# A two-layer decoder trunk on one core: split VectorE sums, ScalarE draining two of eight PSUM banks, a fifth seven-product pair, and a re-ordered opening

## The chip, the cores and the metric

The kernel runs on one core of a Trainium2 chip. TensorE (PE) multiplies, with its weight loads shown as PEld; VectorE (DVE) and ScalarE (ACT) prepare operands and drain PSUM; GpSimd (POOL) and SyncE (SP) start DMA transfers. The metric is the time of one execution in microseconds of device time; lower is better.

## The reference

Two layers on a 256 x 2048 residual stream, all in float32:

```python
def hybrid_layer(x, ...):
    h = rms_norm(x, attn_norm)
    proj = einsum('bsd,de->bse', h, w_in)      # 2048 -> 6160 columns
    ... gated linear attention, stick-breaking attention, norms ...
    x = x + einsum('bse,ed->bsd', mixed, w_o)  # 2048 x 2048
    hm = rms_norm(x, mlp_norm)
    up = square(relu(einsum('bsd,df->bsf', hm, w_up)))   # 2048 x 8192
    return x + einsum('bsf,fd->bsd', up, w_down)         # 8192 x 2048
```

About 500 MB of weights pass once through the core.

## The kernel before

Every large product is done to float32 accuracy with three matmuls: a weight tile is split into a rounded part (`whi`, made by ScalarE at L1091) and the rest (`wlo`, made by VectorE at L1095), the activation likewise, and high x high, high x low and low x high are summed in PSUM (`product`, L1224, L1227, L1228). Below, "product" means one such triple.

Most of the work is a list of **units** (`layer_units`): per layer `g`, `o`, `o`, then four quarters of `up`, `up`, `down`, `down`, and ahead of a layer the three units `iv`, `ik`, `iq` of the next input projection. A unit multiplies 256 rows by a 2048 x 1024 weight block. It goes through eight **pairs** of 128-row weight slices in the order of a table (`EACH`, `OWN`, ...); the second entry of a table names its seven-product pairs, the third those whose split is done by DMA (`chi` by a GpSimd DMA, `dlo` a negated copy made by ScalarE at L1056, to which a second DMA adds the weights). A plain pair costs eight products. A seven-product pair (`fast`, the 2 x 2 Strassen-Winograd scheme) costs seven, but VectorE first forms sums of its weights (`ts`, `raw`, L871) and of its activations (`forms`, L464 to L467). Its products go to PSUM banks m1 to m8, which the unit's **tail** (`seeded_tail`, `up_tail`) adds up on VectorE.

`Plan` decides the order: each piece has a length, its dependences and a due time worked back from TensorE, and VectorE and ScalarE take the ready piece that is due first. The result is the in-order instruction stream of each engine; TensorE's own order is the tables'. In-order means that an instruction that waits holds up all that stand behind it on its engine.

The **opening** is not planned: `unit` runs one 512-column unit `u0` of the first layer (tiles `acc`, `ps`), loading x (`xb`) in four parts between the four weight loads (`raw`, 1 MB each). Then `ordered(-1, ...)` plans `iv`, `ik`, `iq` of layer 0. In the plan, time 0 is five steps (60 matmuls) ahead of the first `iv` product, and VectorE and ScalarE are taken to be free from then on. Weights come through a ring of `RAWS` = 3 `raw` tiles; the first three `chi` tiles are first touched by a one-element ScalarE copy (`held_tile`, L1047), which their DMAs wait for.

Of the kernel before, what the change touches and what calls it, by code (L numbers as in the profile page):

```python
# [14 lines left out]
ALU = mybir.AluOpType  # L15
# [16 lines left out]
OWN = {
    ("up", 0): ([4, 0, 0, 0, 0, 1, 1, 2, 1, 1, 6, 6, 2, 6, 6, 5, 5, 5, 5, 4, 3, 3, 3, 3, 7, 7], (0, 1, 3, 5, 6), (2, 4)),
    ("up", 0, 0): ([0, 0, 1, 1, 1, 4, 4, 1, 3, 3, 3, 6, 6, 3, 2, 6, 6, 5, 5, 5, 5, 2, 7, 7], FAST, (2, 4)),
    ("up", 1): ([0, 0, 3, 3, 3, 3, 2, 1, 1, 1, 2, 1, 5, 5, 5, 4, 6, 5, 6, 6, 6, 7, 4, 7], FAST, (2, 4)),
    ("down", 0): ([0, 0, 3, 3, 1, 2, 3, 3, 1, 1, 5, 1, 4, 5, 5, 5, 2, 6, 6, 6, 6, 7, 7, 4], FAST, (2, 4)),
    ("down", 1): ([0, 0, 5, 5, 4, 5, 5, 6, 6, 6, 4, 6, 3, 3, 3, 1, 2, 3, 1, 1, 1, 2, 7, 7], FAST, (2, 4)),
}
# [23 lines left out]
class Plan:  # L62
# [28 lines left out]
    def run(self):  # L91
# [32 lines left out]
        while events:  # L124
# [9 lines left out]
            for e in free:  # L134
# [38 lines left out]
def trunk_kernel(  # L173
# [275 lines left out]
    def forms(op, i, t, tag):  # L449
# [8 lines left out]

        def sums():
            a11, a21, a12, a22 = (t[:, k, r * P : (r + 1) * P] for k in range(2) for r in range(2))  # L460
            n = 4 if keep else 3
            e.append(tmp("t2", [P, 512], bufs=T2)[:, : n * P].rearrange("p (k c) -> p k c", c=P))
            s = e[0][:, 3, :] if keep else a21
            nc.vector.tensor_tensor(e[0][:, 2, :], a21, a11, ALU.subtract)  # L464
            nc.vector.tensor_tensor(s, a21, a22, ALU.subtract)
            nc.vector.tensor_tensor(e[0][:, 0, :], a11, s, ALU.subtract)
            nc.vector.tensor_tensor(e[0][:, 1, :], a12, e[0][:, 0, :], ALU.subtract)  # L467

# [386 lines left out]
    def ordered(l, units, hT, rst, ug, gates_t, mixed=None, ons=None):  # L855
# [147 lines left out]
        def load(u, i):  # L1003
# [4 lines left out]
            def fn():  # L1008
                if x % RAWS >= 3:
                    box.append(tmp("raw2", [P, 2, 1024], bufs=RAWS - 3))  # L1010
# [9 lines left out]
            if x >= RAWS:  # L1020
                piece.after = raws[x - RAWS]
            raws.append(readers)
# [12 lines left out]
        def rounded(u, j, s):  # L1035
# [252 lines left out]
        def seeded_tail(u):  # L1288
# [18 lines left out]
            def sums(p):  # L1307
# [6 lines left out]
                b = vector(dw, bk(7), dw, a, p[7])  # L1314
                d = vector(x22, bk(5), dw, b, p[5], seeds[8])
                free.update({1: [c], 6: [w], 5: [a, d], 7: [b]})
                box["s"] = (c, b, a, d)

            def half(c, p):
                got = []  # L1320
                for tt, (m, dst) in enumerate((((2, x11), (4, x21)), ((3, x12), (8, x22)))[c]):
                    def fn(m=m, dst=dst, tt=tt):
                        if m == 4:
                            combine(dst(), banks[m], dw(), ALU.subtract)
                        else:
# [4 lines left out]

                    before = [box["s"][2 * c + tt], seeds[m]] + [box["s"][3]] * (m == 4)
                    free[m] = [add("DVE", V1, fn, p[m], before, give=m == 4)]
                    got += free[m]
                x_done[2 * n2 + c] = got
# [3 lines left out]
        def up_tail(u):  # L1338
# [14 lines left out]
            def sums(p):  # L1353
                c = add("ACT", A1, copy, p[1])
                w = add("DVE", V1, new_dw, c, p[6], take=1, sure=1)
                a = vector(y(1, 0), bk(5), lambda: box["w"], w, p[5])
                b = vector(y(0, 1), bk(7), lambda: box["w"], w, a, p[7])
                b.give = 1
                d = vector(y(1, 1), bk(5), y(0, 1), b, p[5])
                free.update({1: [c], 6: [w], 5: [a, d], 7: [b]})  # L1360
                box["s"] = (c, b, a, d)

# [4 lines left out]
            def half(h, p):  # L1367
                box["r", h] = []
                for tt, m in enumerate(((2, 4), (3, 8))[h]):
                    minus = ALU.subtract if (h, tt) == (0, 1) else ALU.add  # L1370
                    before = [box["s"][2 * h + tt]] + [box["s"][3]] * ((h, tt) == (0, 1))
                    a = vector(y(h, tt), bk(m), y(h, tt), p[m], before, op=minus)
                    free[m] = [a]

# [557 lines left out]
```

## Time and profile before

| | |
|---|---|
| median of 3 runs | 2134.3 us (2134.24 to 2135.91) |
| the profiled execution | 2134.41 us, span 2132.7 us |
| busy: PE, PEld, DVE, ACT, POOL | 99%, 83%, 90%, 68%, 13% of the span |
| granted TensorE clock, mean | 0.999 of full speed |
| instructions: PE, DVE, ACT | 10064, 2578, 1940 |
| DMA | 497 MB, mean 233 GB/s |

The profiled execution is 1.7 us longer than its span and 0.1 us above the median. [...]

### The profile page before, as it was taken

What the parts mean: (1) busy time and instruction counts of PE and PEld (TensorE: products, weight loads), DVE (VectorE), ACT (ScalarE), POOL (GpSimd) and SP (SyncE); (2) the same over time, 40 slices, a digit from 0 to 9 for tenths busy, and PEclk for the clock granted to TensorE, in tenths of its full rate; (3) what the DMA queues carried; (4) which work ended last, traced back from release to release, by engine and by line L of the source; (5) the groups of instructions that cost most, each with busy time, mean ns of one, the idle gap of its engine ahead of it and who ended that gap; (6) DMA issues with size and microseconds to landing.
All of it is one profiled execution on the core that took longest, in us unless ns stands there. A gap on an engine that the chain in (4) does not pass through costs nothing.

```text
span 2132.7 us, 28217 instructions
## 1 busy us (share of the span) xinstructions
PE 2120.0 (99%) x10064; PEld 1763.6 (83%) x10064; DVE 1909.1 (90%) x2578; ACT 1452.1 (68%) x1940; POOL 276.4 (13%) x394
## 2 busy tenths in 40 slices
PE   8999999999999999999999999999999999999999
PEld 7888888888888888888888988888888888888887
DVE  5978779999999999999988896799999999999997
ACT  6657667676677677667766575677776776676774
POOL 1110001111111111111111100011112111111110
PEclk9999999999999999999999999999999999999999
DMA  8975358788988988988888644678889788889886
GB/s 257 259 227 174 115 176 242 223 255 243 271 245 244 268 245 245 283 244 234 250 261 245 192 138 138 213 217 244 264 241 272 234 262 256 240 246 273 242 245 200
DMA packets 157617, 497.14 MB, mean 233 GB/s; under 512 B 10682, under 2 KB 19458, under 8 KB 157476
## 3 DMA queue, kind: packets, MB, share of 16 engines
q1 hardware_dynamic: 100900, 319.16, 42.0%
q0 software_dynamic: 56576, 176.18, 36.9%
q8 instruction: 79, 1.29, 0.2%
q14 instruction: 62, 0.51, 0.1%
HBM read 493.20 MB, written 2.10 MB: 232 GB/s over the span
## 4 chain that ended last, share of the span: by engine, by line
PE 94%; DVE 3%; DMA 2%; ACT 1%; issue 1%; SPq 0%; ACTq 0%; DVEq 0%
PE acc L626 3%; PE acc L628 3%; PE acc L627 3%; DVE wlo L1095 1%; DMA xb<-in_x_dram 1%; DMA raw<-in_w_up_dram 1%; DMA raw<-in_w_in_dram 1%; PE ps L1869 0%; PE ps L1862 0%; DVE wlo L609 0%; PE ps L737 0%; PE ps L1819 0%; DVE ts L871 0%; PE ps L791 0%; PE ps L755 0%
## 5 line engine op out<-in xcount | busy, mean ns | idle before, releaser
L1095 DVE TENSOR_TENSOR wlo<-raw,whi 128x1024 fp32r<-128x1024 f32 (+1 forms) x689 | 744.0, 1089 | 86.2 <-ACT whi L1091 39.8
L1091 ACT ACTIVATE whi<-raw 128x1024 fp32r<-128x1024 f32 (+1 forms) x689 | 644.7, 950 | 185.8 <-DVE raw L871 67.6
L1056 ACT ACTIVATE dlo<-chi 128x1024 fp32r<-128x1024 f32 x168 | 177.6, 1057 | 117.7 <-DMA chi<-in_w_o_dram 5.1
L1091 ACT ACTIVATE whi<-ts 128x1024 fp32r<-128x1024 f32 x169 | 179.0, 1059 | 89.9 <-DVE ts L871 42.2
L871 DVE TENSOR_TENSOR ts<-raw 128x1024 f32<-128x1024 f32 x169 | 206.1, 1220 | 6.3 <-DMA raw<-in_w_o_dram 2.4
L1095 DVE TENSOR_TENSOR wlo<-ts,whi 128x1024 fp32r<-128x1024 f32 x169 | 206.1, 1220 | 4.1 <-ACT whi L1091 4.1
L626 PE MATMUL acc<-whi,act 128*128 128x512 f32 (+2 forms) x384 | 141.7, 369 | 1.6 <-ACT whi L607 1.6
L627 PE MATMUL acc<-wlo,act 128*128 128x512 f32 (+2 forms) x384 | 137.1, 357 | 0.2 <-DVE wlo L609 0.2
L628 PE MATMUL acc<-whi,act 128*128 128x512 f32 (+2 forms) x384 | 137.3, 358 | 0.0
L607 ACT ACTIVATE whi<-raw 128x1024 fp32r<-128x1024 f32 (+2 forms) x98 | 88.3, 906 | 69.2 <-PE acc L628 62.4
L609 DVE TENSOR_TENSOR wlo<-raw,whi 128x1024 fp32r<-128x1024 f32 (+2 forms) x98 | 100.3, 1030 | 32.5 <-ACT whi L607 32.3
L871 DVE TENSOR_TENSOR raw<-raw 128x512 f32<-128x512 f32 x169 | 116.2, 688 | 2.3
L871 DVE TENSOR_TENSOR raw<-ts,raw 128x512 f32<-128x512 f32 x169 | 115.8, 685 | 0.6
L1052 POOL DMA_DIRECT2D chi<-in_w_up_dram x64 | 38.0, 594 | 557.9 <-PE m__2856_13480 L1228 30.1
L1052 POOL DMA_DIRECT2D chi<-in_w_down_dram x64 | 38.8, 606 | 498.5 <-PE m__3324_15675 L1228 27.5
L1376 ACT ACTIVATE act<-act,st 128x512 f32<-128x512 f32 x88 | 60.2, 715 | 54.9 <-DVE act L871 54.9
L626 PEld LDWEIGHTS acc<-whi,act 128*128 128x128 f32 x384 | 72.6, 189 | 14.1 <-issue 3.4
L628 PEld LDWEIGHTS acc<-whi,act 128*128 128x128 f32 x384 | 72.7, 189 | 10.6
L627 PEld LDWEIGHTS acc<-wlo,act 128*128 128x128 f32 x384 | 72.8, 190 | 9.4 <-DVE wlo L609 0.5
L1059 POOL DMA_DIRECT2D dlo<-in_w_down_dram x64 | 60.1, 940 | 51.6 <-ACT dlo L1056 48.1
L1059 POOL DMA_DIRECT2D dlo<-in_w_up_dram x64 | 58.3, 912 | 55.9 <-ACT dlo L1056 53.6
L488 DVE TENSOR_TENSOR act<-t,act 128x512 fp32r<-128x512 f32 x92 | 62.7, 685 | 0.0
(4307 smaller groups left out, 5756.4 us busy)
## 6 DMA issues: line engine op xcount, KB each, us to landing
raw<-in_w_up_dram SPq DMA_DIRECT2D x96, 1024.0 KB, 7.4
raw<-in_w_down_dram SPq DMA_DIRECT2D x96, 1024.0 KB, 7.7
raw<-in_w_in_dram SPq DMA_DIRECT2D x72, 1024.0 KB, 5.7
chi<-in_w_up_dram POOLq DMA_DIRECT2D x64, 512.0 KB, 5.6
dlo<-in_w_up_dram POOLq DMA_DIRECT2D x64, 512.0 KB, 8.5
chi<-in_w_down_dram POOLq DMA_DIRECT2D x64, 512.0 KB, 5.6
dlo<-in_w_down_dram POOLq DMA_DIRECT2D x64, 512.0 KB, 8.5
raw<-in_w_o_dram SPq DMA_DIRECT2D x24, 1024.0 KB, 7.5
```

The lines of the kernel that those rows point to most:

```text
L488: nc.vector.tensor_tensor(d[:, :, 1, :], src, f32(d[:, :, 0, :]), ALU.subtract)
L607: newest["hi"] = nc.scalar.activation(h, r, AF.Copy).ins
L609: newest["lo"] = nc.vector.tensor_tensor(lo[:, q : q + step, :width], r, f32(h), ALU.subtract).ins
L626: nc.tensor.matmul(o, xh[:, sl], whi[:, j, :width], start=first, stop=False)
L627: nc.tensor.matmul(o, xh[:, sl], wlo[:, j, :width], start=False, stop=False)
L628: st["mm"] = nc.tensor.matmul(o, xl[:, sl], whi[:, j, :width], start=False, stop=last).ins
L871: nc.vector.tensor_tensor(dst, a, b, op)
L1052: nc.gpsimd.dma_start(flat("h"), src)
L1056: nc.scalar.activation(box["l"], f32(box["h"]), AF.Copy, scale=-1.0)
L1059: nc.gpsimd.dma_start(flat("l"), src, accum_op=ALU.add)
L1091: nc.scalar.activation(box["h"][:, :n], src(), AF.Copy)
L1095: nc.vector.tensor_tensor(box["l"][:, :n], src(), f32(box["h"][:, :n]), ALU.subtract)
```

## The change

Seven things are changed together. (1) Pair 0 becomes a seven-product pair in the second `down` unit of each quarter, whose table then has 26 steps instead of 24; the first `down` unit still uses pair 0 as a plain pair, so both forms of its activations are kept (`TWO_WAYS`, tile `sxk`; the `sxh` one moves to a tile of the `act` pool). (2) The four activation sums of `forms` become four planned pieces instead of one. (3) The planner counts 0.12 us between a VectorE piece and one that depends on it. (4) In both tails ScalarE copies banks m4 and m8 to SBUF, and VectorE adds there; the second read of bank m5 comes after the copy of m8. (5) In the opening the three `held_tile` copies read the last written element of `hT.t[7]`, the last operand of `u0`, instead of the identity, and the planner no longer makes them wait for its first step. (6) The opening's plan has a ring of six weight tiles. (7) Nearly all order tables are new.

```diff
-    ("down", 1): ([0, 0, 5, 5, 4, 5, 5, 6, 6, 6, 4, 6, 3, 3, 3, 1, 2, 3, 1, 1, 1, 2, 7, 7], FAST, (2, 4)),
+    ("down", 1): ([7, 7, 3, 3, 4, 3, 3, 5, 5, 5, 4, 5, 1, 1, 1, 1, 0, 0, 2, 0, 0, 6, 6, 6, 6, 2], (0, 1, 3, 5, 6), (2, 4)),
...
+FIRST_RAWS = 6
...
-                        at[u], free[e] + p.lag + (0.0 if u.engine == e else self.GAP)
+                        at[u], free[e] + p.lag + (self.SAME.get(e, 0.0) if u.engine == e else self.GAP)
...
             if tag_fast:
-                e = add("DVE", 1.25, lambda: part(0), first, take=1, sure=1 + got)
+                for k in range(4):
+                    kw = {} if k else dict(take=1, sure=1 + got)
+                    e = add("DVE", VS, lambda k=k: part(0, k), e, **kw)
...
-                nc.scalar.activation(box["h"][:, 0, :1], ident[:, :1], AF.Copy)
+                nc.scalar.activation(box["h"][:, 0, :1], f32(hT.t[7][:, 1, 1, :1]), AF.Copy)
...
-                first = add("ACT", 0.2, held_tile, before[0])
+                first = add("ACT", 0.2, held_tile)
...
-                d = vector(x22, bk(5), dw, b, p[5], seeds[8])
...
+                    if tt:
+                        free[m] = before = [add(
+                            "ACT", A1,
+                            lambda m=m, dst=dst: nc.scalar.activation(dst(), banks[m], AF.Copy),
+                            before,
+                        )]
+                    if m == 8:
+                        before = vector(x22, bk(5), x22, before, p[5])
+                        free[5] = free[5] + [before]
```

In the built programs TensorE has 24 matmuls fewer (9826 instructions instead of 9850), VectorE 80 instructions more and ScalarE 104 more. Two places matter below.

ScalarE, before, from the last square sums of the opening (`ssq`) on: the three `chi` copies stand at the very start of the program, and the first weight split of `iv` (`whi5`) comes before any `dlo`.

```order
L560 ACTIVATE t2_53_366,ssq_3_95<-xb3_94 128x512
L560 ACTIVATE t2_54_368,ssq_3_95<-xb3_94 128x512
L1091 ACTIVATE whi5_71_410<-raw_65_396 128x1024
L917 ACTIVATE act_55_382<-acc_13_145 128x512
L1056 ACTIVATE dlo_73_418<-chi_66_398 128x1024
```

The same place of the changed program:

```order
L564 ACTIVATE t2_53_366,ssq_3_95<-xb3_94 128x512
L564 ACTIVATE t2_54_368,ssq_3_95<-xb3_94 128x512
L1054 ACTIVATE chi_66_398<-act_43_304 128x1
L1054 ACTIVATE chi_67_400<-act_43_304 128x1
L1054 ACTIVATE chi_68_403<-act_43_304 128x1
L1063 ACTIVATE dlo_71_410<-chi_66_398 128x1024
L1063 ACTIVATE dlo_73_414<-chi_67_400 128x1024
L1098 ACTIVATE whi5_74_418<-raw_65_396 128x1024
L922 ACTIVATE act_55_382<-acc_13_145 128x512
```

The `chi` copies moved behind all ScalarE work of `u0`, and two `dlo` copies, which read what the `chi` DMAs bring, moved ahead of `whi5`.

VectorE, the end of the program (the last unit's tail; `xb3` is the last quarter of the output), before:

```order
L871 TENSOR_TENSOR xb3_94<-m5__4033_18993,t2_4072_19190 128x512
L871 TENSOR_TENSOR xb2_93<-m2__4014_18890,xb2_93 128x512
L871 TENSOR_TENSOR xb2_93<-m4__4018_18928,t2_4072_19190 128x512
L871 TENSOR_TENSOR xb3_94<-m3__4019_18930,xb3_94 128x512
L871 TENSOR_TENSOR xb3_94<-m8__4024_18956,xb3_94 128x512
```

and in the changed program:

```order
L876 TENSOR_TENSOR t2_4128_19428<-m7__4087_19205,t2_4128_19428 128x512
L876 TENSOR_TENSOR xb3_94<-m3__4072_19137,xb3_94 128x512
L876 TENSOR_TENSOR xb2_93<-xb2_93,t2_4128_19428 128x512
L876 TENSOR_TENSOR xb3_94<-m5__4084_19196,xb3_94 128x512
L876 TENSOR_TENSOR xb3_94<-xb3_94,t2_4128_19428 128x512
```

Bank m8 no longer appears here: ScalarE copies it to `xb3` first, and two dependent additions follow instead of one.

## Rows read from the trace of the kernel before

**Rows 1.** The page, busy time (share of the span) and instructions by engine.

```profile
PE 2120.0 (99%) x10064; PEld 1763.6 (83%) x10064; DVE 1909.1 (90%) x2578; ACT 1452.1 (68%) x1940; POOL 276.4 (13%) x394
```

**Rows 2.** Windows, one quarter: us, busy by engine (instructions), clock, DMA share, GB/s.

```profile
617.63:783.78 166.15, 166.15 (x752) 137.93 (x750) 156.85 (x194) 114.35 (x139) 24.75 (x32) 1.00 0.87 252
```

**Rows 3.** Windows of 20 us after the opening unit, same columns.

```profile
40.00:60.00 20.00, 18.89 (x81) 14.63 (x80) 18.43 (x24) 14.94 (x19) 3.72 (x5) 1.00 0.87 209
60.00:80.00 20.00, 19.92 (x87) 15.65 (x86) 19.32 (x31) 13.56 (x18) 3.68 (x5) 1.00 0.98 276
80.00:100.00 20.00, 20.00 (x90) 16.57 (x89) 19.90 (x24) 13.15 (x16) 1.40 (x2) 1.00 0.79 230
...
120.00:140.00 20.00, 18.93 (x83) 15.32 (x83) 19.24 (x24) 12.87 (x15) 1.41 (x2) 1.00 0.70 213
```

**Rows 4.** Timeline, the end: start, length, engine, line, operation [idle before <-releaser].

```profile
2119.10 0.60 ACT L1309 ACTIVATE xb<-m__4041_19027 128x512 f32<-128x512 f32 x1 [0.92 <-PE m__4041_19027 L1228]
...
2121.30 0.69 DVE L871 TENSOR_TENSOR t<-m__4034_18997,t 128x512 f32<-128x512 f32 x1
...
2122.03 0.69 DVE L871 TENSOR_TENSOR xb<-m__4033_18993,t 128x512 f32<-128x512 f32 x1
...
2122.30 0.39 PE L1224 MATMUL m__4024_18956<-chi,act 128*128 128x512 f32 x1
...
2128.20 0.39 PE L1228 MATMUL m__4024_18956<-whi,act 128*128 128x512 f32 x1
2128.62 0.69 DVE L871 TENSOR_TENSOR xb<-m__4024_18956,xb 128x512 f32<-128x512 f32 x1 [0.67 <-PE m__4024_18956 L1228]
```

**Rows 5.** Timeline of VectorE, two stretches without a gap.

```profile
36.10 0.28 DVE L464 TENSOR_TENSOR t<-act 128x128 f32<-128x128 f32 x1
36.30 0.28 DVE L465 TENSOR_TENSOR t<-act 128x128 f32<-128x128 f32 x1
...
46.72 1.22 DVE L1095 TENSOR_TENSOR wlo<-ts,whi 128x1024 fp32r<-128x1024 f32 x1
47.86 0.69 DVE L871 TENSOR_TENSOR raw<-raw 128x512 f32<-128x512 f32 x1
48.46 1.22 DVE L1095 TENSOR_TENSOR wlo<-raw,whi 128x1024 fp32r<-128x1024 f32 x1
```

**Rows 6.** The chain that ended last: start, us, what (two PSUM additions).

```profile
404.86 1.20 DVE xb L871 x2
```

**Rows 7.** Timeline of TensorE in the opening.

```profile
10.26 0.51 PE L626 MATMUL acc<-whi,act 128*128 128x512 f32 x1 [1.56 <-ACT whi L607]
...
11.91 0.63 PE L627 MATMUL acc<-wlo,act 128*128 128x512 f32 x1
...
14.89 0.48 PE L628 MATMUL acc<-whi,act 128*128 128x512 f32 x1
...
16.05 1.09 PE L503 MATMUL ps<-ident,xb 128*128 128x128 f32 x8 [0.68 <-DMA xb<-in_x_dram]
...
38.29 0.39 PE L1224 MATMUL m__80_432<-whi,act 128*128 128x512 f32 x1
```

**Rows 8.** Window in the opening, columns as in Rows 2.

```profile
12.00:14.00 2.00, 2.00 (x6) 1.58 (x5) 0.79 (x2) 0.63 (x1) 0.00 (x0) 0.50 1.06 398
```

**Rows 9.** Timeline of ScalarE in the opening.

```profile
33.79 1.13 ACT L1091 ACTIVATE whi<-raw 128x1024 fp32r<-128x1024 f32 x1
38.49 0.60 ACT L917 ACTIVATE act<-acc 128x512 f32<-128x512 f32 x1 [3.57 <-PE acc L628]
38.99 1.05 ACT L1056 ACTIVATE dlo<-chi 128x1024 fp32r<-128x1024 f32 x1
```

**Rows 10.** Timeline of GpSimd in the opening.

```profile
2.63 1.77 POOL L1052 DMA_DIRECT2D chi<-in_w_in_dram  x3 [1.24 <-ACT chi L1047]
```

**Rows 11.** DMA issues of the first 60 us: count, KB each, median us to landing.

```profile
chi<-in_w_in_dram POOLq DMA_DIRECT2D x5, 512.0 KB, 7.7
```

**Rows 12.** The page, DMA issues, same columns.

```profile
chi<-in_w_up_dram POOLq DMA_DIRECT2D x64, 512.0 KB, 5.6
```

More of the change, by code (lines that the diff above doesn't have):

```diff
@@ L32 @@
 OWN = {
[L33 to L36, printed above, removed]
-    ("down", 1): ([0, 0, 5, 5, 4, 5, 5, 6, 6, 6, 4, 6, 3, 3, 3, 1, 2, 3, 1, 1, 1, 2, 7, 7], FAST, (2, 4)),
+    ("up", 0): ([2, 5, 5, 5, 5, 1, 1, 1, 1, 2, 0, 0, 0, 3, 4, 0, 3, 3, 3, 6, 4, 6, 6, 6, 7, 7], (0, 1, 3, 5, 6), (2, 4)),
@@ L38 @@
+    ("up", 0, 0): ([0, 0, 3, 4, 3, 3, 1, 3, 4, 1, 1, 1, 5, 5, 2, 5, 5, 6, 6, 2, 6, 6, 7, 7], FAST, (2, 4)),
+    ("up", 1): ([7, 7, 5, 5, 4, 5, 5, 1, 1, 1, 2, 3, 1, 3, 3, 3, 4, 6, 6, 6, 6, 0, 2, 0], FAST, (2, 4)),
+    ("down", 0): ([0, 0, 1, 1, 1, 3, 4, 1, 3, 5, 3, 3, 4, 5, 5, 5, 2, 6, 6, 6, 6, 7, 7, 2], FAST, (2, 4)),
+    ("down", 1): ([7, 7, 3, 3, 4, 3, 3, 5, 5, 5, 4, 5, 1, 1, 1, 1, 0, 0, 2, 0, 0, 6, 6, 6, 6, 2], (0, 1, 3, 5, 6), (2, 4)),
 }
 CAST, AHEAD_BY = 3, 1
+FIRST_RAWS = 6
 RING, LOWS, ADDS, RAWS = 5, 4, 2, 3
@@ L71 @@
     GAP = 0.06
+    SAME = {"DVE": 0.12}
     class Piece:
@@ L457, in forms, with new, sums @@
         todo = []
[L459 to L467, printed above, removed]
+        a11, a21, a12, a22 = (t[:, k, r * P : (r + 1) * P] for k in range(2) for r in range(2))
+        def new(k):
+            if not e:
+                n = 4 if keep else 3
+                e.append(tmp("t2", [P, 512], bufs=T2)[:, : n * P].rearrange("p (k c) -> p k c", c=P))
+            return a21 if k == 3 and not keep else e[0][:, k, :]
+        def sums(k):
+            a, b = ((a21, a11), (a21, a22), (a11, new(3)), (a12, new(0)))[k]
+            nc.vector.tensor_tensor(new((2, 3, 0, 1)[k]), a, b, ALU.subtract)
         def high():
@@ L860, in ordered @@
         open_scope("sbuf", mlp=1)
+        slots = RAWS if l >= 0 else FIRST_RAWS
         hm = Operand()
@@ L1008, in fn @@
             def fn():
-                if x % RAWS >= 3:
-                    box.append(tmp("raw2", [P, 2, 1024], bufs=RAWS - 3))
+                if x % slots >= 3:
+                    box.append(tmp("raw2", [P, 2, 1024], bufs=slots - 3))
                 else:
@@ L1019, in load @@
             piece = add("SP", 2.9, fn, lag=LAND)
-            if x >= RAWS:
-                piece.after = raws[x - RAWS]
+            if x >= slots:
+                piece.after = raws[x - slots]
             raws.append(readers)
@@ L1314, in sums @@
                 b = vector(dw, bk(7), dw, a, p[7])
-                d = vector(x22, bk(5), dw, b, p[5], seeds[8])
-                free.update({1: [c], 6: [w], 5: [a, d], 7: [b]})
-                box["s"] = (c, b, a, d)
+                free.update({1: [c], 6: [w], 5: [a], 7: [b]})
+                box["s"] = (w, b, a, b)
             def half(c, p):
@@ L1321, in half @@
                 for tt, (m, dst) in enumerate((((2, x11), (4, x21)), ((3, x12), (8, x22)))[c]):
+                    before = [p[m], seeds[m]]
+                    if tt:
[7 more added lines that the diff above has]
+                        free[5] = free[5] + [before]
                     def fn(m=m, dst=dst, tt=tt):
-                        if m == 4:
-                            combine(dst(), banks[m], dw(), ALU.subtract)
+                        if tt:
+                            combine(dst(), dst(), dw(), ALU.subtract if m == 4 else ALU.add)
                         else:
@@ L1329, in fn @@
                             nc.sync.dma_start(ov[:, tt, n * 512 : (n + 1) * 512], xb[n][:, tt, :])
-                    before = [box["s"][2 * c + tt], seeds[m]] + [box["s"][3]] * (m == 4)
-                    free[m] = [add("DVE", V1, fn, p[m], before, give=m == 4)]
-                    got += free[m]
+                    users = box.setdefault("users", []) if tt else []
+                    got.append(add("DVE", V1, fn, before, box["s"][2 * c + tt], users, give=len(users)))
+                    users.append(got[-1])
+                    if not tt:
+                        free[m] = got[-1:]
                 x_done[2 * n2 + c] = got
@@ L1353, in sums @@
             def sums(p):
-                c = add("ACT", A1, copy, p[1])
+                c = box["c"] = add("ACT", A1, copy, p[1])
                 w = add("DVE", V1, new_dw, c, p[6], take=1, sure=1)
                 a = vector(y(1, 0), bk(5), lambda: box["w"], w, p[5])
[L1357 to L1361, printed above, removed]
+                b = vector(lambda: box["w"], bk(7), lambda: box["w"], w, a, p[7])
+                free.update({1: [c], 6: [w], 5: [a], 7: [b]})
+                box["s"] = (w, b, a, b)
             into = kind not in AHEAD
@@ L1369, in half @@
                 for tt, m in enumerate(((2, 4), (3, 8))[h]):
[L1370 to L1373, printed above, removed]
+                    before = p[m]
+                    if tt:
+                        free[m] = before = [add(
+                            "ACT", A1,
+                            lambda m=m, h=h: nc.scalar.activation(
+                                box[h][:, 1, :], banks[m], AF.Copy
+                            ),
+                            before, box["c"],
+                        )]
+                    if m == 8:
+                        before = vector(y(1, 1), bk(5), y(1, 1), before, p[5])
+                        free[5] = free[5] + [before]
+                    users = box.setdefault("users", []) if tt else []
+                    a = vector(
+                        y(h, tt), y(h, tt), (lambda: box["w"]) if tt else bk(m), before,
+                        box["s"][2 * h + tt], users, op=ALU.subtract if m == 4 else ALU.add,
+                    )
+                    a.give = len(users)
+                    users.append(a)
+                    if not tt:
+                        free[m] = [a]
                     def relu(tt=tt):
```

22 lines of the change are left out of this document (11 added, 11 removed).

## The prediction

> **What bounds the kernel now.** First the page's busy shares: TensorE 99% of the span, VectorE 90%, ScalarE 68% [rows 1]. Then the windows, which show where the missing per cent lies. A whole quarter has TensorE busy for all of its 166.15 us, VectorE for 156.85 [rows 2]: there only fewer matmuls shorten anything, and VectorE has 9.3 us idle in which to take more work. The reader is to see that "busy" hides slow stretches: a full window holds 90 matmuls, three windows after the opening 81, 87 and 83 [rows 3], so 9 + 3 + 7 = 19 slots were lost there. Last the timelines, for the price of a step. A matmul costs (2128.20 - 2122.30) / 26 = 0.227 us from start to start [rows 4], so those 19 slots are 4.3 us. VectorE's own price is also start to start, shorter than the length shown: 1.14 us for 1024 columns, 0.60 for 512, 0.20 for 128 [rows 5]; but 0.73 for 512 when the next instruction reads its output [rows 4], 0.13 more.
>
> **The seven-product pair.** 24 matmuls fewer, all in stretches where TensorE never waits: 24 x 0.227 = 5.4 us gained. The bounds are 5.4 and nothing, should VectorE then set the pace. So its load is needed. Per quarter the pair adds on the weight side one `ts` and one more full `wlo` (2 x 1.14), two half sums and a half `wlo` (3 x 0.60), and on the activation side four sums (4 x 0.20) and about one more `low` (0.60): 2.3 + 1.8 + 0.8 + 0.6 = 5.5 us.
>
> **Counting dependent steps.** In the built orders 453 VectorE instructions stood directly behind the one whose tile they read, 304 do now; in one quarter 29 and 17. Twelve fewer at 0.13 us give back 1.6 us. The load per quarter goes from 156.85 to about 160.8 us, in 166.15 - 0.7 = 165.5 us: 97%, with 4.7 us idle instead of 9.3. The cover of all this work is that idle time. It is worst in the second `up` unit, where the counted instructions come to some 43 us in TensorE's 42.5, but they did before as well, and no wait showed. I take nothing for new waits; bounds: 1 us gained (the new tables may end small waits at the start of a layer's plan), 4 us lost (0.5 us per quarter).
>
> **ScalarE drains two banks.** Eighty VectorE additions read SBUF where they read PSUM. The rows show no gain: 0.60 us each from PSUM [rows 6] and 0.60 from SBUF [rows 5]. [...] The 80 copies (0.60 us each [rows 4]) are 6 us per quarter on ScalarE, which has 166.15 - 114.35 = 51.8 us free [rows 2]. What is late is the last bank: m8 ends with the unit's last product, and then come a copy and two dependent additions, and bank m5, which the next unit's transposes need, is free only after the first of them: 0.60 + 0.73 = 1.3 us, against 12 matmuls (2.7 us) of the next unit's first step. Hidden, except behind a VectorE backlog of more than 1.4 us, and except at the very end of the program, where nothing follows. There one addition (0.69 us from 2128.62 [rows 4]) becomes copy 0.60, hand-over 0.05, addition 0.73, addition 0.69: 1.4 us lost.
>
> **The opening.** Three parts.
> (a) Before, POOL started three `chi` transfers at 2.63 us [rows 10], 1.57 MB, among the first loads of x and weights; DMA was full at some 398 GB/s [rows 8]. TensorE waited for x at 16.05 [rows 7]. Without `chi` those bytes are 1.57 / 0.398 = 4.0 us of DMA time, so the second part of x, and all behind it up to the end of `u0`, come about 4.0 us earlier: `u0` ends near 34.3, not 38.3 [rows 7], and ScalarE's last square sum near 29.8, not 33.8 [rows 9]. Bounds: 3 and 4.7 us, of which the second goes with an undisturbed clock.
> (b) Then the new order bites. ScalarE touches the `chi` tiles only now; the first transfer starts at 30.2, the second at 30.8. A `chi` transfer took 5.6 us to land in the median of a quarter's traffic [rows 12], 7.7 in the opening [rows 11], where the weight loads shared the engines, as they will again: SP then has three to four 1 MB loads outstanding (six tiles). The second of two in one queue may take 1.3 us longer (0.52 MB at 398 GB/s). So the second `chi` lands between 36.4 and 39.8; I take 38.1, the middle, since SP's backlog is part run down by then. ScalarE stands at `dlo<-chi` until then, and behind it stand `whi5`, which the first product needs, both copies of `u0`'s result and every further `whi`; VectorE waits for `whi5` in its turn. Then `dlo` and `whi5`, 1.05 us each with 0.1 overlap [rows 9], put the first `iv` matmul at 40.1 (38.4 to 41.8) against 38.29: 1.8 us lost (0.1 to 3.5). Its second matmul needs `wlo`, one VectorE instruction of 1.22 us more: 1.0 us lost. [...]
> (c) TensorE idles from 34.3 to 40.1. [...]
> Against that stand the 4.3 us of lost slots after 40 us. They came from a VectorE without lead and from a weight load that landed late, and six tiles and the pause itself cure both; I leave 0.5 us of them. The opening in sum: +1.8 + 1.0 + 1.6 - 4.3 + 0.5 = +0.6 us, from -3.2 (early `chi`, no slow stretch, no slot lost) to +3.9 (late `chi`, two).
>
> **The sum.** 2134.4 of the profiled execution - 5.4 + 1.4 + 0.6 = 2131.0 us. The three runs have a median of 2134.3, so the forecast in their terms is 2130.9, 0.16% less. The measurement tells 0.2%, 4.3 us, from no change; so this counts as no change.
>
> **Rivals.**
> *The opening gains in full.* `chi` lands by 36.5, the clock stays up or dips unseen during the pause. Then the opening gives -2.3 to -3.2 us and the total is 2127 to 2128. For it: the loads of SP may have run out by 33 us; 5.6 us is the common landing time [rows 12]. Against it: the 7.7 us of the opening [rows 11], and the clock's fall after a far shorter pause [rows 8]. [...]
> *VectorE becomes the bound (slower).* Its 9.3 us of idle time per quarter are in part forced, by waits for ScalarE's `whi` and TensorE's banks. At most 4.7 us may stay. It decides from 5.7 us on: eight quarters with 1.0 us each would cost 8 us, and the total is 2139, slower than before; if all 9.3 stay, 8 x 4.6 = 37 us, 2168. Against it: an engine that runs late finds its inputs ready, so its idle time shrinks by itself; one window of the present trace has VectorE busy for 19.90 of 20 us beside a full 90 matmuls [rows 3]. For it: `wlo` has only four tiles, so a late tail on VectorE starves TensorE within some 5 us.
> *The pair doesn't shorten anything.* VectorE paces just the second `down` units; the 0.7 us per quarter go into waits: 2130.9 + 5.4 = 2136.3, no change either.
>
> **Chances.** The forecast (2130.0 to 2133.5): 0.42. The opening gains in full, or partly so that the total is under 2130.0: 0.38. The pair lost, or a worse opening (2133.5 to 2138.6): 0.13. VectorE the bound, over 2138.6: 0.07. Faster by over 0.2% is thus 0.38, within 0.2% 0.55, slower 0.07. The range takes in the opening's bounds and 1 us on the units' side: down to 2126.0, up to 2135.5, outside of which I leave some 0.15.
>
> **What would show it.** In the changed profile: 24 matmuls fewer; quarters of about 165.5 us with TensorE busy throughout and VectorE near 160.8; the x transposes of 16.05 near 12; `u0`'s end near 34; ScalarE idle before `dlo<-chi`, released by the `chi` transfer, for 6 to 9 us; the first `iv` matmul near 40 with a granted clock of 0.50 behind it; windows from there to 140 us with full counts; and about 1.4 us more between the last matmul and the end. Wrong would be: quarters longer than 166 us, TensorE waiting for `wlo` within them, or no pause after `u0`.

## The result and the profile after

The changed kernel takes 2145.57 us (median of 4 runs, 2141.03 to 2146.8) where the kernel before takes 2134.27: a ratio of 1.0050, 95% interval 1.0038 to 1.0062. The forecast of 2130.9 and its range were too low. The profiled execution took 2145.65 us, its span is 2144.0 us, 11.3 more than before. In the experiments below, one execution of e3 (3052.44 us) and one of e6 (9709.13 us) were far slower than the others of the same kernel and are left out of the medians.

First the page's busy times and one whole quarter, from the same product to the same product as in [rows 2].

```profile
PE 2117.9 (99%) x10040; PEld 1762.7 (82%) x10040; DVE 1936.9 (90%) x2658; ACT 1509.6 (70%) x2044; POOL 279.1 (13%) x394
```

```profile
627.57:793.16 165.59, 165.59 (x748) 137.23 (x747) 160.46 (x204) 120.69 (x150) 25.65 (x32) 1.00 0.88 255
```

TensorE issues 24 matmuls fewer, the quarter is 0.56 us shorter, TensorE is busy throughout, and VectorE carries 160.46 us of work. So the loss lies elsewhere. The waits of TensorE, longest in total first (who waited for whom, us in total, times, longest), name three places:

```profile
PE m__86_446 L1231 <- ACT whi L1098: 8.1, 1, 8.1
PE m__230_1143 L1231 <- DVE act L876: 4.2, 1, 4.2
PE acc L630 <- DVE act L876: 4.2, 2, 2.7
```

**The opening.** The timelines of ScalarE and of TensorE:

```profile
29.82 0.48 ACT L1054 ACTIVATE chi<-act 128x1 fp32r<-128x1 f32 x3
37.76 1.06 ACT L1063 ACTIVATE dlo<-chi 128x1024 fp32r<-128x1024 f32 x1 [7.46 <-DMA chi<-in_w_in_dram]
40.14 1.06 ACT L1063 ACTIVATE dlo<-chi 128x1024 fp32r<-128x1024 f32 x1 [1.32 <-DMA chi<-in_w_in_dram]
41.10 1.04 ACT L1098 ACTIVATE whi<-raw 128x1024 fp32r<-128x1024 f32 x1
```

```profile
33.68 0.39 PE L632 MATMUL acc<-whi,act 128*128 128x512 f32 x1
42.20 0.79 PE L1231 MATMUL m__86_446<-whi,act 128*128 128x512 f32 x1 [8.13 <-ACT whi L1098]
43.46 0.79 PE L1234 MATMUL m__86_446<-wlo,act 128*128 128x512 f32 x1 [0.47 <-DVE wlo L1102]
```

`u0` ends 4.4 us earlier than before, but ScalarE stands at the two `dlo` until 40.14, and the first `iv` matmul comes at 42.20 instead of 38.29 [rows 7]. The windows show what follows (columns as in [rows 2]; the first is the half-clock stretch, the others answer to [rows 3]):

```profile
37.29:47.53 10.24, 4.87 (x11) 3.49 (x12) 5.35 (x7) 7.50 (x9) 1.77 (x2) 0.50 0.92 204
```

```profile
60.00:80.00 20.00, 20.00 (x90) 16.54 (x89) 18.57 (x33) 13.87 (x20) 2.82 (x4) 1.00 0.89 247
80.00:100.00 20.00, 20.00 (x90) 16.58 (x89) 15.93 (x20) 10.21 (x13) 1.97 (x3) 1.00 0.84 273
...
120.00:140.00 20.00, 15.53 (x61) 12.06 (x60) 12.55 (x16) 9.22 (x12) 1.40 (x2) 0.91 0.91 288
```

The window at 60 us, which had lost three slots, is full now, with 90 matmuls; the one at 80 us was full before as well. The last one has 61: 29 slots lost, 29 x 0.227 = 6.6 us, against 7 slots before.

**The start of `iq`.** What happens there, on VectorE and on TensorE:

```profile
116.31 4.45 DVE L1102 TENSOR_TENSOR wlo<-raw,whi 128x1024 fp32r<-128x1024 f32 x4
128.20 1.23 DVE L876 TENSOR_TENSOR ts<-raw 128x1024 f32<-128x1024 f32 x1 [7.45 <-DMA raw<-in_w_in_dram]
...
131.08 0.68 DVE L876 TENSOR_TENSOR act<-act,m__158_802 128x512 f32<-128x512 f32 x1
```

```profile
131.90 0.47 PE L1231 MATMUL m__230_1143<-whi,act 128*128 128x512 f32 x1 [4.21 <-DVE act L876]
```

VectorE waits 7.45 us for one weight load. Behind it, in order, stand the additions of the previous unit's tail; the one at 131.08 reads the bank that TensorE needs. The DMA issues between 108 and 122 us (count, KB each, median us to landing) and the waits of SP's queue from 60 to 131 us show why the load is late:

```profile
raw<-in_w_in_dram SPq DMA_DIRECT2D x4, 1024.0 KB, 14.8
```

```profile
SPq L1023 <- DVE wlo L1102: 43.0, 7, 21.8
```

SP stood up to 21.8 us at one tile of the ring that wasn't free, issued one load at 105.27 and four more between 112.2 and 119.8. The trace has the landing of one of these four, issued at 113.42: it took 14.8 us, and it is the load that VectorE waits for.

**From a plan to the attention.** The end of the last projection unit ahead of layer 1's attention, on TensorE and ScalarE, and VectorE's next read of m5 (`m__2278`); `m__2271` is bank m8:

```profile
1207.69 0.39 PE L1235 MATMUL m__2271_10683<-whi,act 128*128 128x512 f32 x1
1210.77 0.39 PE L630 MATMUL acc<-whi,act 128*128 128x272 f32 x1 [2.69 <-DVE act L876]
```

```profile
1208.18 1.33 ACT L1410 ACTIVATE act<-act,st 128x512 f32<-128x512 f32 x2 [0.76 <-DVE act L876]
1209.42 0.57 ACT L1391 ACTIVATE act<-m__2271_10683 128x512 f32<-128x512 f32 x1
```

```profile
1210.02 0.69 DVE L876 TENSOR_TENSOR act<-m__2278_10722,act 128x512 f32<-128x512 f32 x1
```

```profile
1211.48:1214.89 3.41, 3.41 (x17) 3.41 (x16) 2.22 (x5) 1.37 (x2) 0.00 (x0) 0.50 0.46 147
```

The next matmul is no transpose of a following unit but `acc`, whose PSUM tile lies over the banks of the plan. It waits for the second read of m5, which comes behind the copy of m8: 2.69 us here and 1.47 us at the first such place (176.04), and here a half-clock stretch follows. The kernel before, at the same place (`m__2242` is its m8):

```profile
1199.77 0.28 PE L626 MATMUL acc<-whi,act 128*128 128x272 f32 x1
```

```profile
1199.97 0.69 DVE L871 TENSOR_TENSOR act<-m__2242_10568,act 128x512 f32<-128x512 f32 x1
```

There `acc` starts right behind the last product, ahead of VectorE's read of m8, so the bank that it needs is not m8; VectorE's second read of m5 had started at 1195.00.

**The end** has the copy and the two dependent additions that the prediction named:

```profile
2138.54 0.60 ACT L1332 ACTIVATE xb<-m__4076_19160 128x512 f32<-128x512 f32 x1 [2.12 <-PE m__4076_19160 L1235]
```

```profile
2139.17 0.69 DVE L876 TENSOR_TENSOR xb<-m__4084_19196,xb 128x512 f32<-128x512 f32 x1
2139.89 0.69 DVE L876 TENSOR_TENSOR xb<-xb,t 128x512 f32<-128x512 f32 x1
```

Cut at the starts of TensorE's first matmul of each stage (from the timelines; e8 and e10 are experiments below), the span divides so:

| stage, us | before | after | e8 | e10 |
|---|---|---|---|---|
| start to first `iv` matmul | 38.29 | 42.20 | 38.22 | 34.96 |
| `iv`, `ik`, `iq` | 126.64 | 133.84 | 124.15 | 124.30 |
| attention, layer 0 | 131.05 | 131.22 | 131.05 | 131.08 |
| units of layer 0, next projection | 903.79 | 903.51 | 900.44 | 900.81 |
| attention, layer 1 | 152.23 | 153.87 | 152.22 | 152.22 |
| units of layer 1 | 776.20 | 773.47 | 773.23 | 773.71 |
| last matmul's start to the end | 4.49 | 5.84 | 5.56 | 5.55 |

The first row also differs from execution to execution: with the opening of before the first `iv` matmul starts at 38.29 (before) and 39.11 (e7), with that of e8 at 38.22 (e8) and 39.46 (e9).

### The profile page after: what moved, and what is told of

The parts are those of the page before. It is cut to its first block, busy times and chain, and to the rows that moved or that the text cites. A ratio compares the mean times of both kernels' runs of the same rounds, so it can differ in the third digit from the quotient of the medians.

```text
span 2144.0 us, 28336 instructions
## 1 busy us (share of the span) xinstructions
PE 2117.9 (99%) x10040; PEld 1762.7 (82%) x10040; DVE 1936.9 (90%) x2658; ACT 1509.6 (70%) x2044; POOL 279.1 (13%) x394
## 4 chain that ended last, share of the span: by engine, by line
PE 91%; DVE 3%; ACT 3%; DMA 2%; issue 1%; POOL 0%; ACTq 0%; DVEq 0%
PE acc L630 3%; PE acc L632 3%; PE acc L631 3%; DMA raw<-in_w_in_dram 1%; DVE wlo L1102 1%; ACT whi L611 0%; DMA raw<-in_w_o_dram 0%; ACT whi L1098 0%; DMA chi<-in_w_in_dram 0%; PE ps L1903 0%; DVE wlo L613 0%; PE ps L1896 0%; DVE act L876 0%; PE ps L741 0%; PE ps L1853 0%
## 5 line engine op out<-in xcount | busy, mean ns | idle before, releaser
L1098 ACT ACTIVATE whi<-ts 128x1024 fp32r<-128x1024 f32 x177 | 187.3, 1058 | 70.0 <-DVE ts L876 33.9
L876 DVE TENSOR_TENSOR ts<-raw 128x1024 f32<-128x1024 f32 x177 | 215.5, 1218 | 11.3 <-DMA raw<-in_w_in_dram 8.6
L1102 DVE TENSOR_TENSOR wlo<-ts,whi 128x1024 fp32r<-128x1024 f32 x177 | 215.3, 1216 | 1.8 <-ACT whi L1098 1.7
L876 DVE TENSOR_TENSOR raw<-raw 128x512 f32<-128x512 f32 x177 | 121.1, 684 | 1.8
L876 DVE TENSOR_TENSOR raw<-ts,raw 128x512 f32<-128x512 f32 x177 | 120.7, 682 | 0.1
L1066 POOL DMA_DIRECT2D dlo<-in_w_down_dram x64 | 65.3, 1020 | 151.9 <-ACT dlo L1063 123.5
```

Of the source, the lines that this page charges most:

```text
L876: nc.vector.tensor_tensor(dst, a, b, op)
L1066: nc.gpsimd.dma_start(flat("l"), src, accum_op=ALU.add)
L1098: nc.scalar.activation(box["h"][:, :n], src(), AF.Copy)
L1102: nc.vector.tensor_tensor(box["l"][:, :n], src(), f32(box["h"][:, :n]), ALU.subtract)
```

## The experiments

Times are medians; the kernel before gave 2134.04 to 2134.24 us beside them.

**e1: `chi` early again**, all else as changed.

```diff
-                nc.scalar.activation(box["h"][:, 0, :1], f32(hT.t[7][:, 1, 1, :1]), AF.Copy)
+                nc.scalar.activation(box["h"][:, 0, :1], ident[:, :1], AF.Copy)
...
-                first = add("ACT", 0.2, held_tile)
+                first = add("ACT", 0.2, held_tile, before[0])
```

> The changed kernel with the chi copies of the opening back at the start of the program (they read the identity again). Theory A, the late chi transfers cost the opening's time: TensorE has no pause of 8 us after u0, the first iv matmul starts near 38.3 us instead of 42.2, and the half-clock stretch behind it goes; 5 to 6 us less than the changed kernel, so 2139.5 to 2140.5. The waits for bank m5 at the two ends of a plan (1.6 and 2.8 us) stay. Rival B, the loads that chi displaces come as much later as the pause was long (u0 ends near 38 again and x waits near 16): within 2 us of the changed kernel, 2143.5 or more. If the 4.4 us wait near 127 us is an effect of the late start of the chi queue, it goes too, and the time is near 2135.

Measured: 2138.26 us (2134.07 to 2139.55), 7.3 less than the changed kernel. The first `iv` matmul starts at 38.31, the waits for `acc` stay at 4.2 us in all, the wait at the start of `iq` is 2.3 us. Theory A holds; 1 to 2 us more are gained, since in this execution the load at `iq` landed in 12.7 us instead of 14.8 and no half-clock stretch followed (granted clock 1.00 from 124 to 132 us).

**e2: three weight tiles and the old table** for `iv`, `ik`, `iq`.

```diff
-EACH = [0, 0, 1, 1, 1, 2, 7, 3, 3, 3, 3, 2, 5, 5, 5, 5, 4, 1, 6, 6, 6, 4, 6, 7], FAST, (2, 4)
+EACH = [7, 7, 5, 2, 5, 5, 1, 1, 5, 4, 1, 1, 3, 3, 3, 3, 4, 6, 6, 2, 6, 6, 0, 0], FAST, (2, 4)
-FIRST_RAWS = 6
+FIRST_RAWS = 3
```

> The changed kernel with three weight tiles in the opening and the order table of iv, ik and iq of the kernel before. The chi order of the change stays. Theory A, the wait of 4.4 us near 127 us comes from the six-tile ring and its table (freed in bursts, loads of 14.8 us on full DMA engines): it goes, and with it the half-clock stretch behind it, 5 to 6 us less, near 2140. Rival B, it comes from VectorE's later tails, whatever the ring: a wait of 3 us or more remains at the start of iq and the time is within 2 us of 2145.6. Rival C: with three tiles the pause after u0 grows, since fewer loads are ahead, and the time is longer than 2146.

Measured: 2140.32 us, 5.3 less than the changed kernel. No wait is left at the start of `iq`; the pause after `u0` remains, and the waits for `acc` grow to 5.9 us. Theory A holds. The pause is 6.8 us instead of 8.1, so Rival C fell: with three tiles less is under way (248 GB/s from 20 to 40 us, 397 in the changed kernel), and `chi` lands sooner (7.6 us in the median of three, 8.9 in the changed kernel).

**e3: the old tails** under the new tables, and **e4: the new pair alone** in the kernel before. In both, nothing makes the first addition of a tail wait for the sum that still reads its operand, so a part of the result may be another; e11 adds that order, and the conclusions rest on it.

```diff
-                box["s"] = (w, b, a, b)
+                d = vector(x22, bk(5), dw, b, p[5], seeds[8])
+                free.update({1: [c], 6: [w], 5: [a, d], 7: [b]})
+                box["s"] = (c, b, a, d)
...
+                    free[m] = [add("DVE", V1, fn, p[m], before, give=m == 4)]
```

> The changed kernel with the two tails of the kernel before: no ScalarE copies of m4 and m8, bank m5 read early again. Theory A, the late read of m5 holds the first acc product of the attention: the waits of 1.6 us near 174 and 2.8 us near 1208 go, with the half-clock stretch behind the second (1.4 us), and the program ends 1.4 us sooner: 7 us less than the changed kernel, near 2138.5. The pause after u0 and the raw wait near 127 stay. Rival B, these waits come from a VectorE that is behind by its new work: they stay with another releaser, and only the 1.4 us at the end are won, near 2144.

```diff
-    ("down", 1): ([0, 0, 5, 5, 4, 5, 5, 6, 6, 6, 4, 6, 3, 3, 3, 1, 2, 3, 1, 1, 1, 2, 7, 7], FAST, (2, 4)),
+    ("down", 1): ([7, 7, 3, 3, 4, 3, 3, 5, 5, 5, 4, 5, 1, 1, 1, 1, 0, 0, 2, 0, 0, 6, 6, 6, 6, 2], (0, 1, 3, 5, 6), (2, 4)),
...
+TWO_WAYS = (("sxh", 0), ("sx", 0))
```

> The kernel before with the seven-product pair of the second down unit alone (its new table, both forms of the activations kept for it); opening, tails, planner and all other tables as before. Theory A, 24 matmuls fewer in stretches where TensorE never waits: 5.4 us less than before, 2128.9. Rival B, VectorE sets the pace of these units without the other edits: no gain, 2134 or more, with TensorE waiting for wlo in the down units.

Measured: e3 2164.58, e4 2171.14 us. All four theories fell. The waits for `acc` do vanish in e3, but TensorE now waits for VectorE's additions behind the second `down` unit of seven quarters: 2.3 to 3.1 us each in e3, 3.3 to 3.6 in e4. This suggests that the new table and the ScalarE copies belong together, which I had not seen; e11 tests it alone.

**e5: old-style tails at two places only**, the last projection unit of a plan (`iq`) and the program's last unit.

```diff
+            last = kind == "iq"
...
-                    if tt:
+                    if tt and not last:
...
+                    if last:
+                        a = vector(
+                            y(h, tt), bk(m), y(h, tt), before, box["s"][2 * h + tt],
+                            [box["s"][3]] * (m == 4), op=ALU.subtract if m == 4 else ALU.add,
+                        )
```

> The changed kernel, in which only two of its tails go back to direct VectorE additions from m4 and m8 with m5 read early: that of iq, the last unit of each plan ahead of the attention, and that of the program's last unit. Theory A, the late read of m5 holds the first acc product: both waits (1.6 us near 174, 2.8 near 1208) go, the half-clock stretch of 3.4 us behind the second goes (1.4 us), and the end is 1.4 us shorter: 7.3 us less than the changed kernel, near 2138.3. Pause after u0 and raw wait near 127 stay as they are. Rival B, VectorE is behind by its other new work at these places: the acc products still wait 1.5 us or more each, only the end is won, near 2144.

Measured: 2136.48 us (2132.8 to 2139.45), 9.1 less than the changed kernel. The list of waits has no `acc` row for VectorE any more. Theory A holds for the hand-over. It missed at the end, which is only 0.3 us shorter (5.57 us); e9 shows why. The wait at `iq` is 0.2 us in this execution: the load was issued 1.9 us sooner than in the changed kernel and landed in 12.2 us instead of 14.8.

**e6: the pair in the kernel before, under a table with room for the old tail.**

```diff
+    ("down", 1): ([4, 0, 0, 0, 0, 5, 5, 4, 5, 5, 6, 6, 6, 6, 3, 3, 3, 1, 2, 3, 1, 1, 1, 2, 7, 7], (0, 1, 3, 5, 6), (2, 4)),
```

> The kernel before with the fifth seven-product pair in the second down unit, under a table of which the last three entries are no products of a seven-product pair (it ends 2, 7, 7, and the last such pair is over four steps before the end, as in the tables of before). Tails, opening, planner as before. Theory A, the pair is worth its 24 matmuls where the tail has room: 2128.9, no wait of TensorE for VectorE at the start of the units behind it. Rival B, VectorE cannot carry the pair: waits of over 1 us for wlo or for a bank in each quarter, 2134 or more.

Measured: 2159.93 us. It doesn't tell the theories apart: no wait for a bank stands out in the `down` units, but the pair by DMA at the table's start brought waits of up to 3.7 us for `dlo<-in_w_down_dram`. The table is bad for another reason; e9 answers the question.

**e7: the changed tails alone** in the kernel before (the whole functions `seeded_tail` and `up_tail` of the change; two of their lines):

```diff
+                    if m == 8:
+                        before = vector(x22, bk(5), x22, before, p[5])
+                        free[5] = free[5] + [before]
```

> The kernel before with the changed tails alone (ScalarE copies m4 and m8, m5 read behind the copy of m8); all tables, the opening and the planner's costs as before. Theory A, the late m5 is paid where a plan hands over to the attention: waits of 1.5 to 3 us for acc near 165 and 1200, with or without a half-clock stretch of 1.4 us behind each, and 1.4 us at the end: 2138 to 2142. Rival B, the price that the prediction named (1.4 us at the end and nothing else): 2135.7. Rival C, the banks m4 and m8 come free sooner and TensorE waits less somewhere: 2134 or less.

Measured: 2142.66 us, ratio 1.0040 (1.0025 to 1.0055). Theory A. The first wait of its list, and the window behind the first of the two places:

```profile
PE acc L626 <- DVE act L871: 4.9, 2, 3.2
```

```profile
167.00:171.00 4.00, 3.21 (x14) 3.21 (x15) 2.96 (x7) 1.13 (x5) 0.00 (x0) 0.50 0.47 131
```

4.9 us of waits, and a half clock at the longer one, by which the attention of layer 0 takes 133.66 instead of 131.05 us; at the end 5.84 us instead of 4.49. Rival B, my own price, is refuted. Of the 8.4 us over before, 0.8 lie in the opening, ahead of any tail. The copies also gain something: TensorE's wait of 1.1 us at the start of `iq` in the kernel before is gone here.

**e8: the three repairs together**: the edits of e1, e2 and e5 in the changed kernel.

```diff
-FIRST_RAWS = 6
+FIRST_RAWS = 3
...
+                first = add("ACT", 0.2, held_tile, before[0])
...
+            last = kind == "iq"
```

> The changed kernel with its three repairs together: chi copies back at the start, three weight tiles and the old table for iv, ik and iq, and the two tails of e5. Theory A, the losses add up and nothing else is wrong: e1 gave 2138.3, less 7.3 of the tails, less 2.5 of the wait at the start of iq that e1 still has: 2128.5, faster than before by 0.27%. Rival B, one cause lies deeper (a VectorE that has lost its lead) and the waits come back at another place: 2132 or more.

Measured: 2127.25 us (2126.5 to 2128.49), ratio to before 0.9966 (0.9955 to 0.9978). Theory A: no new wait takes the place of the old ones, and the change without them is faster. Singly the repairs gained 7.3, 5.3 and 9.1 us, 21.7 in sum, together 18.3; they overlap at the start of `iq`, where e1 and e5 had shorter waits too. Two windows of e8, columns as in [rows 2]:

```profile
60.00:80.00 20.00, 20.00 (x90) 16.42 (x89) 19.38 (x30) 13.12 (x18) 3.68 (x5) 1.00 1.01 296
120.00:140.00 20.00, 20.00 (x90) 16.58 (x89) 19.93 (x24) 14.06 (x18) 1.41 (x2) 1.00 0.72 212
```

Both had lost slots before. They are full here with three tiles, the old table of these units and no pause after `u0`. In e7, the changed tails alone, the one at 120 us has 90 matmuls as well, that at 60 us 86.

**e9: e8 without the pair.**

```diff
-    ("down", 1): ([7, 7, 3, 3, 4, 3, 3, 5, 5, 5, 4, 5, 1, 1, 1, 1, 0, 0, 2, 0, 0, 6, 6, 6, 6, 2], (0, 1, 3, 5, 6), (2, 4)),
+    ("down", 1): ([0, 0, 5, 5, 4, 5, 5, 6, 6, 6, 4, 6, 3, 3, 3, 1, 2, 3, 1, 1, 1, 2, 7, 7], FAST, (2, 4)),
...
-TWO_WAYS = (("sxh", 0), ("sx", 0))
+TWO_WAYS = (("sxh", 0),)
```

> The combined kernel (e8) without the fifth seven-product pair: the second down unit has the table of before again, four such pairs and 24 steps, and its pair 0 is plain. Theory A, with repaired hand-overs the pair is worth exactly its 24 matmuls: 5.4 us more than e8's 2127.25, so 2132.7. Rival B, VectorE pays part of it back in waits, and the pair is worth 3 us or less: 2130.3 or less.

Measured: 2132.45 us, 5.2 more than e8. In the two stages of layer units the difference is (903.05 - 900.44) + (776.31 - 773.23) = 5.7 us. Theory A: the pair is worth its 24 matmuls, but for the end of the program. There e8 takes 5.56 us and e9 4.49: under the new table the last seven-product pair ends late, and in e8 eight additions stand in VectorE's queue from 2116.41 on. The first and the last of the eight:

```profile
2116.41 0.69 DVE L876 TENSOR_TENSOR t<-m__4095_19236,xb 128x512 f32<-128x512 f32 x1 [3.16 <-PE m__4095_19236 L1235]
...
2120.73 0.68 DVE L876 TENSOR_TENSOR xb<-m__4076_19156,xb 128x512 f32<-128x512 f32 x1
```

So the late end of the changed kernel has two causes, the copy of m8 and this queue, and e5 took away only the first.

**e10: e8 with the `chi` copies in the middle of the opening's ScalarE work.**

```diff
+    def touch():
+        for _ in range(CAST):
+            first_chi.append(tmp("chi", [P, 2, 512], F32R, bufs=CAST))
+            nc.scalar.activation(first_chi[-1][:, 0, :1], f32(hT.t[4][:, 1, 1, :1]), AF.Copy)
+
+    after(5, touch)
```

> The combined kernel (e8), but the three chi copies stand in the middle of the opening's ScalarE work (near 24 us, behind the second pair of square sums and the last operand's copies) instead of at its start or behind its end. Theory A, the price of the late start and that of the early one are both avoidable: x comes early as in the changed kernel, u0 ends near 34 us, chi lands by 33, the first iv matmul starts at 34.5 to 35.5 without a half-clock stretch: 2.5 to 3.5 us less than e8, near 2124. Rival B, the DMA engines are full until 36 us (some 400 GB/s), so the bytes of chi come out of the first weight tile of iv or of u0's last one: the first iv matmul is at 37 or later and the time within 1 us of e8's 2127.25.

Measured: 2124.07 us (2123.83 to 2124.32), ratio to before 0.9954 (0.9939 to 0.9969), the fastest of all. ScalarE, then TensorE:

```profile
24.51 0.48 ACT L1700 ACTIVATE chi<-act 128x1 fp32r<-128x1 f32 x3
...
31.59 1.06 ACT L1065 ACTIVATE dlo<-chi 128x1024 fp32r<-128x1024 f32 x1 [1.54 <-DMA chi<-in_w_in_dram]
32.91 1.06 ACT L1065 ACTIVATE dlo<-chi 128x1024 fp32r<-128x1024 f32 x1 [0.26 <-DMA chi<-in_w_in_dram]
```

```profile
33.43 0.39 PE L632 MATMUL acc<-whi,act 128*128 128x512 f32 x1
34.96 0.51 PE L1231 MATMUL m__83_440<-whi,act 128*128 128x512 f32 x1 [1.14 <-ACT whi L1098]
```

Issued 5.3 us earlier, the same transfers hold up neither x nor `u0`, and the first `iv` product only a little: ScalarE waits 1.54 and 0.26 us for them, TensorE 1.14 us for ScalarE.

**e11: e8 with direct additions from m4 and m8 in all tails.**

```diff
+                d = vector(x22, bk(5), dw, b, p[5], seeds[8])
+                free.update({1: [c], 6: [w], 5: [a, d], 7: [b]})
+                box["s"] = (w, b, a, d)
```

> The combined kernel (e8) with direct VectorE additions from m4 and m8 in all tails, not only in the two of e8 (the first addition of each tail also waits for the sum that reads its operand). Theory A, the new table of the second down unit, which ends its last seven-product pair one step before the end, needs the ScalarE copies: they free m4 and m8 while VectorE is still behind with eight additions. Without them the unit behind each of the seven or eight down units waits 2 to 4 us for m4 or m3: 2145 to 2160. Rival B, the copies free nothing that is waited for (as the prediction took it): within 2 us of 2127.25.

Measured: 2151.52 us, 24.3 more than e8. TensorE and VectorE of e11 behind one `down` unit (`m__1071` is m4, `m__1080` m8), then ScalarE of e8 at the same place (m4, m8):

```profile
574.79 0.50 PE L1231 MATMUL m__1150_5440<-chi,act 128*128 128x512 f32 x1 [1.87 <-DVE xb L876]
```

```profile
574.05 0.69 DVE L876 TENSOR_TENSOR xb<-m__1071_5072,t 128x512 f32<-128x512 f32 x1
...
576.99 0.69 DVE L876 TENSOR_TENSOR xb<-m__1080_5110,xb 128x512 f32<-128x512 f32 x1
```

```profile
567.88 0.60 ACT L1337 ACTIVATE xb<-m__1071_5069 128x512 f32<-128x512 f32 x1
...
570.60 0.60 ACT L1337 ACTIVATE xb<-m__1080_5127 128x512 f32<-128x512 f32 x1 [1.17 <-PE m__1080_5127 L1235]
```

Theory A: VectorE comes to m4 only at 574.05 and to m8 at 576.99, where ScalarE in e8 has copied m4 by 568.5 and m8 by 571.2. In each of seven quarters TensorE waits 1.4 to 1.9 us for m4, 12.7 us in all; half-clock stretches follow two of these waits (near 1083 and 1810 us), and the rest is in smaller waits that I have not ascribed.

**e12: e8 with the six tiles and the new table of the change.**

```diff
-FIRST_RAWS = 3
+FIRST_RAWS = 6
-EACH = [7, 7, 5, 2, 5, 5, 1, 1, 5, 4, 1, 1, 3, 3, 3, 3, 4, 6, 6, 2, 6, 6, 0, 0], FAST, (2, 4)
+EACH = [0, 0, 1, 1, 1, 2, 7, 3, 3, 3, 3, 2, 5, 5, 5, 5, 4, 1, 6, 6, 6, 4, 6, 7], FAST, (2, 4)
```

> The combined kernel (e8) with the six weight tiles and the new table for iv, ik and iq of the change. Theory A, the wait of VectorE and ScalarE for one weight load (issued near 110 us, landing 12 to 15 us later) and TensorE's wait at the start of iq belong to this ring and table: they come back, 2 to 4 us more than e8 and a wider spread, 2129.5 to 2131.5. Rival B, the wait near 127 was a consequence of the late chi transfers or of the tails: gone here too, 2127 to 2128.

Measured: 2134.04 us (2129.84 to 2138.2), 6.8 more than e8. Theory A in kind, its 2 to 4 us too small. The DMA issues from 100 to 125 us in e12, and in e8, with three tiles:

```profile
raw<-in_w_in_dram SPq DMA_DIRECT2D x4, 1024.0 KB, 15.5
```

```profile
raw<-in_w_in_dram SPq DMA_DIRECT2D x4, 1024.0 KB, 6.8
```

Each figure is the landing of one load, the only one of the four whose landing the trace has. In e12 the four go out between 106.6 and 115.7 us, in e8 between 102.4 and 118.8. The burst and TensorE's wait (4.0 us) are back without the late `chi` and with the repaired hand-over, so neither causes them. e12 changes ring and table together; which of the two makes the burst is open. No run tries changes (2) and (3) of the list, or the other new tables, alone.

## Why the prediction was wrong, by its own steps

**The seven-product pair**: right. 5.4 us forecast, 5.2 measured between e9 and e8; 5.7 in the layer units, of which 1.1 go back at the end.

**Counting dependent steps**: right in its result; no run has this term by itself. 160.46 us of VectorE per quarter (160.8 forecast), quarters of 165.59 us (165.5), no wait within them. VectorE did not become the bound.

**ScalarE drains two banks**: this step failed, twice. Its price for the end was right (1.35 us in e7, 1.4 forecast); the hand-over in it, put at 0.05 us, took 0.03 in the changed kernel (ScalarE's copy ends at 2139.14, VectorE's read starts at 2139.17). But "hidden" was worked out for one follower of the tail alone, the next unit's transposes with 12 matmuls as cover. At the end of a plan the follower is `acc`, with no matmul as cover: the copy of m8, VectorE's read of m5, and whatever stands in the queues between them lie on TensorE's path. e7 has the tails alone: 8.4 us over before, some 7.6 of them behind the opening, where the step had 1.4. And the gain side was put at nothing because an addition costs 0.60 us from either source ([rows 5], [rows 6]). That is not what the copies do: they free m4 and m8 without VectorE's queue, and the new table of the second `down` unit needs that; without them the kernel takes 24.3 us more (e11).

**The opening**: (a) was right, `u0`'s last matmul starts at 33.68. In (b) the mechanism was right and the landing mis-sized: the two `chi` that ScalarE waits for were issued at 30.4 and 31.1 and landed just ahead of 37.76 and 40.14, after 7.3 and 8.9 us, the second above its bound of 39.8; the first `iv` matmul came at 42.20, above its bound of 41.8. The engines were full meanwhile (407 GB/s from 34 to 37.29 us), and the rival that the opening gains in full, with `chi` landed by 36.5, fell. Between 95 and 125 us, where the engines were not always full (66 GB/s from 95 to 100 us), the shortest of four `chi` transfers of the same kernel landed in 3.8 us. In (c) the 1.6 us were my estimate for one half-clock stretch: eight matmuls at 0.20 us more than 0.227, since behind the wait of 1.56 us, at a clock of 0.50 [rows 8], matmuls started 0.43 us apart [rows 7]. No run shows 1.6 us behind the pause; the changed kernel lost 2.0 us there: after 43.46 nine matmuls started 0.42 to 0.59 us apart, the pause having taken half of the stretch. The term that failed is the last one, "six tiles and the pause itself cure both". At 120 us the six tiles with their table made the largest single loss, 29 slots where 0.5 us had been left for all places. And they are not the cure: e8, with neither six tiles nor the pause, has full windows at 60 and 120 us; at 120 us the changed tails alone suffice (e7), at 60 us the runs leave open what does it. Ring and table cost 6.8 us (e12 against e8), where the term had a gain of 3.8.

**The sum.** Rows and runs leave no large part untold: of the 11.3 us, 3.9 arise before the first `iv` matmul, 7.2 in `iv` to `iq` (two half-clock stretches, the waits of 4.2 and 1.5, less the slots won back at 60 us), 0.2 and 1.6 in the two attentions, 1.35 at the end, and the layer units give back 0.3 + 2.7, the first figure after its own `acc` wait of 2.7. Not all of this is a fixed price: the 1.6 come from a half-clock stretch behind the wait of 2.69 us, and in e2 the same wait at the same place had none (last section). The three repairs (e1, e2, e5) bring 2145.57 down to 2127.25, and e10, which keeps the early x as well, to 2124.07: 10 us under the kernel before.

## What to carry to other kernels

When a buffer is freed later, list every follower that may take it over, at the end of a stage above all, and price each with its own cover; a bound found at one follower says nothing of the next. Price a drain by when it frees its bank and in whose queue it stands, not only by its length. A deeper ring is no lead by itself: here, with its new table, one tile was held long, the in-order queue stood behind it (up to 21.8 us), and the loads then went out close together (four between 112.2 and 119.8 us); a late load held up whatever stood behind it on the engine that waited (VectorE, 7.45 us).

## What the runs showed of the hardware

A 1 MB weight load took 6.8 us to land (e8, issued at 108.74) and 15.5 us (e12, issued at 107.76) in the same stretch of the program. The first was issued 6.4 us behind another load of that size, the second 1.2 us; that this spacing makes the difference is my reading; no run has it alone.

The length of TensorE's idle time alone did not decide on the clock. The same `acc` product waited 2.69 us in the changed kernel (1210.77) and in e2:

```profile
1207.34 0.39 PE L630 MATMUL acc<-whi,act 128*128 128x272 f32 x1 [2.69 <-DVE act L876]
```

In the changed kernel the clock fell to 0.50 shortly after the work had begun again (at 1211.48), for 3.4 us; in e2 it stayed at 1.00 (1200 to 1220 us). Of the seven waits of 1.4 to 1.9 us in e11, two were followed by such a stretch (0.53 from 1082.2 to 1084 us, 0.50 from 1809.4 to 1812.4). In the pause of 8.1 us the clock fell from 1.00 to 0.50 at 37.29, while TensorE was idle, and 5 of its 10.24 us lay in the pause.
